# Two transformer-like blocks on one core: gelus in one batch, w8 low parts as differences, three weight pieces prepared at fixed steps

## The chip, the cores and the metric

The kernel runs on one core of a Trainium2 chip (trn2). A core has five engines that run side by side, each with its own queue of instructions: TensorE (PE: matmuls, with PEld for the loads of its weights), VectorE (DVE), ScalarE (ACT), GpSimd (POOL) and SyncE (SP, which here only issues transfers). Data lies in HBM, in SBUF (128 partitions) and in PSUM, where matmuls put their sums in eight banks of 128x512 floats. The metric is the device time of one launch in microseconds; lower is better.

## The reference

All arrays are float32, the sequence has 512 tokens and 1024 channels. The first block (hybrid attention and a gated feed-forward layer) is not touched. What matters of the second block:

```python
h = _rms(x, norm1_w) * (1 + sc1) + sh1
u, q, k, v = split(h @ w_in)                  # 512, 512, 128, 128 columns
# _s5: a state-space scan over the tokens, 32 groups of 16 channels
y = C(scan(u)) + d_skip * u
z = gelu(y)
y_ssm = z * sigmoid(z @ w_glu + b_glu)
# _swa_sink: attention in a window of 128 tokens, 8 q heads, 2 kv heads
y_attn = softmax_with_sink(rms(q) @ rms(k).T + bias) @ v
x = x + g1 * (concat(_rms(y_ssm), _rms(y_attn)) @ w_out)
h2 = _rms(x, norm2_w) * (1 + sc2) + sh2
up = causal_conv3(h2 @ w_up) + conv_b         # 2 x 2816 columns
val, gate = split(up)
x = x + g2 * ((silu(gate) * val) @ w_down)
```

## The kernel before, in words

Activations lie with channels on the partitions and the 512 tokens along them. A product in float32 is made of three matmuls in a faster format (`fp32r`): each operand is split into a high part (`hi`, the rounded value) and a low part (`lo`, the rest), and `mm3` adds hi·hi, hi·lo and lo·hi in PSUM. So each weight has to be split before its use. The weights come in pieces of 128x1024 floats (512 KB), in one queue over the whole kernel: w6 is w_glu (2 pieces here called for by steps `g`), w7 is w_out (8 pieces), w8 is w_up (44 pieces) and w9 w_down.

A piece is prepared by `_Lazy.load` (L366). `fetch` has SP issue the transfer from HBM to a `raw` buffer (L356; there are two, `NRAW`). ACT copies `raw` to `whi`, which rounds it (L374). The low part comes in one of two ways. For weights named in `DMA_LO` (w6, w7 and w8), ACT writes the negated rounded copy to `wlo` (L377) and POOL issues a transfer that fetches the same weights from HBM a second time and adds them to it (L378). For the others, w9 and those of the first block among them, DVE subtracts `whi` from `raw` (L381). There are five `whi` and five `wlo` buffers (`NHL`). A step that uses a piece (`pieces`, `get`) also has the next one loaded (`AHEAD` is 1). Before the second feed-forward block `hold_after` stops this, and `go_on` lets it run again once the normalised halves `hl` are issued (L1366 on ACT, L1367 on DVE).

The first part of the second block interleaves the state-space layer and the attention. The string `ORDER` names its steps one after another, and PE runs them in that order. `a`, `b`, `c`, `d` are the stages of the scan, one number for each quarter of the channels. Step `d` puts a quarter of y in PSUM; `copy("y2", ...)` moves it to SBUF (`ys`, on ACT or DVE by a letter in the string `EN`), eight transfers write it to DRAM in another layout (`d_z`; five of them queued on ACT, three on SP, by `ZQ`), and a transfer on POOL reads it back as `yt`. Step `e` applies gelu to the quarters and splits them into `zhl` (ACT copy L507, DVE subtraction L508): with `EG` at 0, `e0` does quarters 0 and 1 and `e1` quarters 2 and 3. `kp`, `kt`, `qp`, `qt` project and transpose k and q (with a norm: Ln L512, Exp L513, then DVE L533). `s` makes the scores of one window and their softmax (DVE L1598, ACT Exp L1603 and L1605), `t` transposes the probabilities (PE L1616, then a copy `pt`), `v` multiplies by v, and `g` is the gated product with w6 and a tanh (L1643). `R`, `A` are norms, `p` and what follows are the products with w7.

Gelu, tanh and the Ln/Exp pair need different activation tables of ACT. A change of table is an ACT_TABLE_LOAD row; `tables` (L308 to L311) asks for the Ln/Exp table again.

ORDER binds PE alone. The other engines are ordered by a planner that schedules the same instructions by estimated costs, except within `high_priority` and where `issue_after` ties an instruction behind another. So a change in one step moves rows of ACT, DVE, SP and POOL elsewhere.

After the last w7 products `norm_tail` normalises the residual in two halves of the tokens; its square sums end in `rsq` (L519, L520). `start_ffn2` (L1690) then begins the second feed-forward block with three w8 groups, `first8`, in PSUM banks `acc`; later groups go round `tr`, `sc` and `acc`. `conv_ff` (ACT L1717, DVE L1719) takes each group out of PSUM with the causal convolution, `hidden2` applies silu and the product (L1727). w8 and w9 chunks alternate; `d` in `hd` is the hidden layer.

Of the kernel before, what the change touches and what calls it, by code (L numbers as in the profile page):

```python
# [11 lines left out]
AF = mybir.ActivationFunctionType  # L12
# [27 lines left out]
TAIL = 4  # L40
ZQ = "assssaaa"
HP = ""
EG = 0
EN = "avaaavaaaaaaaaaaaaavvvvvvvavavvaaaavaaaaaaaaaaaavaavvvvavvvvaaaavvvvaavvvaaaaavavaaavaavvavvvvvvvvvvavvaavvvvvavvaaavaaaavaaavvaaaaaaavvvvvvvaaaaaaaaavvvavvaavaaaav"
EN_AT = {'k1': (0, 4), 'v1': (4, 4), 'q1': (8, 12), 'h1': (20, 8), 'w1': (28, 8), 's1': (36, 8), 'o1': (44, 16), 't1': (60, 46), 'u2': (106, 4), 'z2': (110, 4), 'y2': (114, 4), 'k2': (118, 2), 'v2': (120, 2), 'q2': (122, 4), 'h2': (126, 12), 's2': (138, 12), 't2': (150, 14)}
ORDER = "U kp0 kp1 a0 a1 kt0 b0 qp0 c0 a2 b1 qp1 kt1 b2 c1 d0 a3 c2 qt0 qt1 b3 c3 d1 s0 qp2 s1 s2 t0 d2 t1 d3 e0 s3 e1 qt2 t2 s4 qp3 v0 t3 s5 v1 g0 qt3 g1 g2 t4 g3 s6 v2 v3 s7 t5 R p0 p1 v4 p2 t6 v5 p3 p4 v6 t7 p5 v7 p6 p7 A"
NW = 16
NHL = 5
SUM_E = "vector"
DMA_LO = ("w6", "w7", "w8")  # L50
LAG = 4
NRAW = 2
NW2 = 19
# [179 lines left out]
def build(tc, I, out, PV, PVN, CS, CSN, CS1, CSN1):  # L233
    nc = tc.nc
    st = ExitStack()
    act = nc.scalar.activation
# [3 lines left out]
    def by(cat, n):  # L240
        o, w = EN_AT[cat]
        assert n < w
        return EN[o + n]

    def copy(cat, n, dst, src, scale=None):

        if by(cat, n) == "a":
            return act(dst, src, AF.Copy) if scale is None else act(dst, src, AF.Copy, scale=scale)  # L248
        if scale is None:
            return V.tensor_copy(dst, src)  # L250
        return V.tensor_scalar(dst, src, scale, None, op0=ALU.mult)
# [8 lines left out]
    def mm(o, l, r, start, stop, **k):  # L260
        nc.tensor.matmul(o, lhsT=l, rhs=r, start=start, stop=stop, **k)  # L261
# [11 lines left out]
    def acc():  # L273
        return pacc.tile([P, 512], F32, tag="acc", name="acc")
# [20 lines left out]
    def V1(n, k=None):  # L295
        o, w = PV[n]
        return pv[:, o:o + w] if k is None else pv[:, o + k:o + k + 1]
# [7 lines left out]
    def tables(after=None, name="natural_log_exp_and_others"):  # L305

        if after is None:
            nc.scalar.preload_act_table_set(name)  # L308
        else:
            with tc.issue_after(after.ins if hasattr(after, "ins") else after):  # L310
                nc.scalar.preload_act_table_set(name)  # L311
# [27 lines left out]
    class _Lazy:  # L339
# [27 lines left out]
        def load(self):  # L367
# [5 lines left out]
            for a, b in self.halves():  # L373
                act(v(hi)[:, a:b], v(raw)[:, a:b], AF.Copy)  # L374
            if self.name in DMA_LO:
                k0, k1, c0, c1 = self.cut
# [7 lines left out]
    wpieces, queue, limit = {}, [], [1 << 30]  # L384
# [113 lines left out]
    def hl():  # L498
        return hlp.tile([P, 2, S], F32R, tag="hl", name="hl")
# [856 lines left out]
    a1 = cpool.tile([P, 16], F32, name="a1")  # L1356
# [36 lines left out]
    a2 = ExitStack()  # L1393
    bp = a2.enter_context(tc.tile_pool(name="attn2", bufs=1, reuse_waits="tile"))

    def wt(nm):
        return bp.tile([P, S], F32, tag="w", bufs=NW2, name=nm)
# [4 lines left out]
    zT, zhl = [], []  # L1402
    zs, z2s, cs, ss, sps, ets, tts, gts = {}, {}, {}, {}, {}, {}, {}, {}

    def s5_load(qs):
        for q in qs:
            ets[q] = tab("et")
            nc.sync.dma_start(ets[q], d_et[q])
            cs[q], ss[q] = wt("co"), wt("si")
            nc.sync.dma_start(cs[q], d_rot[q][:, 0])  # L1410
            nc.sync.dma_start(ss[q], d_rot[q][:, 1])
# [9 lines left out]
    s5_load2((0, 1))  # L1421
    s5_load((2, 3))

    def u_out(q, ps):
        t = wt("uT").rearrange("p (s c) -> p s c", s=8)
        copy("u2", q, t, ps.rearrange("p (c s) -> p s c", s=8))
        nc.scalar.dma_start(d_u[q // 2][q % 2 * 8:q % 2 * 8 + 8].rearrange("g h s c -> (g h) (s c)"), t.rearrange("p s c -> p (s c)"))
# [3 lines left out]
    v2 = bp.tile([P, NT, 128], F32, name="v2")  # L1431
# [15 lines left out]
    def u_last():  # L1447
        for q in range(3):
            u_out(q, group[q][0])
        u_load(0)  # L1450
        ps = acc()
        proj_f(ps, wu[1], h, 1)
        u_out(3, ps)
        u_load(1)
# [25 lines left out]
    def s5_c(q):  # L1480
        if q == 2:
# [8 lines left out]
        V.tensor_tensor(sp[:, :, 1:65], z.rearrange("p (g c) -> p g c", g=8),  # L1490
                        zc.rearrange("p (g c) -> p g c", g=8), op=ALU.add)

    def s5_d(q):
        ut = wt("ut")
        nc.gpsimd.dma_start(ut, d_u[q // 2][q % 2 * 8:q % 2 * 8 + 8].rearrange("g h s c -> (g h) (s c)"))
        py = acc()
        for g in range(8):
            mm(py[:, g * 64:g * 64 + 64], tts[q][:, g * P:(g + 1) * P], ua[:, q * 8 + g], True, False)
            mm(py[:, g * 64:g * 64 + 64], gts[q][:, g, 16:144], sps[q][:, g, 0:64], False, True)
        ys = wt("ys").rearrange("p (g c) -> p g c", g=8)  # L1500
        copy("y2", q, ys.rearrange("p g c -> p (g c)"), py)
        for t in range(8):
            E = {"g": nc.gpsimd, "a": nc.scalar, "s": nc.sync}[ZQ[t]]
            E.dma_start(d_z[q].rearrange("g h t c -> t h g c")[t], ys[16 * t:16 * t + 16])
        yt = xp.tile([P, S], F32, tag="x", name="yt")
        nc.gpsimd.dma_start(yt, d_z[q].rearrange("g h t c -> (g h) (t c)"))
        V.scalar_tensor_tensor(yt, ut, V1("ssm_d", q), yt, op0=ALU.mult, op1=ALU.add)
        zT.append(yt)

    def s5_e(n):  # L1510
        if EG and n == 0:
            return
        for q in (range(4) if EG else (2 * n, 2 * n + 1)):
            ge = act(zT[q], zT[q], AF.Gelu_apprx_tanh)
            zz = hl()
            split(zz, zT[q])
            zhl.append(zz)
        tables(ge)
# [139 lines left out]
    def ssm_out(k):  # L1658
# [5 lines left out]
        V.scalar_tensor_tensor(t, ps, gm[:, k:k + 1], r_s, op0=ALU.mult, op1=ALU.mult)  # L1664
        G.tensor_tensor(x[k], x[k], t, op=ALU.add)

    steps = dict(U=u_last, a=s5_a, b=s5_b, c=s5_c, d=s5_d, e=s5_e, kp=kv_p, kt=kv_t, qp=q_p, qt=q_t,
                 s=swa_s, t=swa_t, v=swa_v, g=glu, R=norm_s, p=ssm_out, A=norm_a)
    with tc.manual_schedule(engines={mybir.EngineType.PE}):
        for step in ORDER.split():  # L1670
            name = step.rstrip("0123456789")
# [71 lines left out]
def _make(inputs):  # L1743
    import concourse.bacc as _bacc

    arrays = arrays_of(inputs)
    PV, PVN = _offsets(pvec(inputs))
    CS, CSN = _offsets(consts_of(False))
    CS1, CSN1 = _offsets(consts_of(True))
    nc = _bacc.Bacc("TRN2", target_bir_lowering=False, num_devices=1)  # L1750
    ins, feed = {}, {}
    for name, a in arrays.items():
        ins[name] = nc.dram_tensor(f"in_{name}_dram", a.shape, F32, kind="ExternalInput").ap()
        feed[f"in_{name}_dram"] = a
    out = nc.dram_tensor("out_0_dram", (D, S), F32, kind="ExternalOutput").ap()
    with tile.TileContext(nc) as tc:
        build(tc, ins, out, PV, PVN, CS, CSN, CS1, CSN1)
    return nc, feed
# [8 lines left out]
```

## Time and profile before

| | |
|---|---|
| three runs | 1284.62, 1287.53, 1288.72 us (median 1287.53) |
| the profiled execution | 1290.43 us, its span 1288.6 us |
| PE busy | 1230.1 us (95%), 6269 matmuls |
| DVE busy | 836.3 us (65%) |
| ACT busy | 553.8 us (43%) |
| POOL busy | 312.1 us (24%) |
| read from HBM | 178.22 MB |

The span is the time between the first and the last instruction of the profiled execution; 1.8 us of its own time lie around it. The busy shares are means over stages that differ: attention of the first block up to some 300 us, its feed-forward layer up to 680, state space and attention of the second block up to about 880, its feed-forward layer after 900. What a stage loses is read in that stage, from the waits of PE.

### The profile page before, as it was taken

To read this page: it belongs to the slowest core of one execution; us is meant where nothing else is said; L and a number is where in the kernel's file an instruction comes from. 1 tells how busy PE (TensorE), PEld (TensorE's weight loads), DVE (VectorE), ACT (ScalarE), POOL (GpSimd) and SP (SyncE) were. 2 spreads that over 40 slices of the span, in tenths; PEclk is the share of its full clock that TensorE was granted. 3 is DMA by queue.
4 is the path that set the end of the run, shared out by engine and by line. 5 is a ranking of instruction groups with operands and counts; after the bars stand their busy time and mean duration, and the time that the engine had idled before them with its cause. 6 is when DMAs were issued, how large, how long until landed. Compare 5 with 4: busy or idle time off the path is not lost.

```text
span 1288.6 us, 17279 instructions
## 1 busy us (share of the span) xinstructions
PE 1230.1 (95%) x6269; PEld 993.0 (77%) x6269; DVE 836.3 (65%) x1622; ACT 553.8 (43%) x918; POOL 312.1 (24%) x399
## 2 busy tenths in 40 slices
PE   7899999999999999999999978889899999999998
PEld 6788765667887878888889877668777788888886
DVE  7668868677977967676667488756547343434362
ACT  6334465454332323232325235765655544444430
POOL 1000004113409283755201331032121211111200
PEclk9999999999999999999999887989899999999999
DMA  6431111126356665666547865457799989796921
GB/s 223 156 112 49 51 33 50 50 61 191 115 162 202 218 200 181 188 194 198 176 144 248 246 150 129 122 129 129 140 209 194 211 168 161 148 177 141 186 82 66
DMA packets 211156, 192.95 MB, mean 150 GB/s; under 512 B 13056, under 2 KB 173712, under 8 KB 211072
## 3 DMA queue, kind: packets, MB, share of 16 engines
q1 hardware_dynamic: 154528, 146.96, 37.8%
q0 software_dynamic: 51456, 40.61, 19.8%
q10 hardware_dynamic: 5088, 4.29, 1.0%
q8 instruction: 50, 0.82, 0.3%
q14 instruction: 34, 0.28, 0.1%
HBM read 178.22 MB, written 15.43 MB: 150 GB/s over the span
## 4 chain that ended last, share of the span: by engine, by line
PE 76%; DVE 9%; issue 5%; DMA 5%; ACT 4%; POOL 1%; SPq 0%; POOLq 0%; DVEq 0%; ACTq 0%
PE acc L261 51%; PE sc L261 12%; PE tr L261 8%; DMA raw<-in_w_dram 3%; PE po L261 2%; DMA wlo<-in_w_dram 2%; DVE wlo L381 1%; PE tr L886 1%; ACT whi L374 1%; DVE z L1478 1%; DVE z L1467 1%; PE tr L1616 1%; DVE z L1466 1%; POOL keep L929 0%; POOL wlo L378 0%
## 5 line engine op out<-in xcount | busy, mean ns | idle before, releaser
L261 PE MATMUL acc<-hl,whi 128*128 128x512 f32 (+1 forms) x1624 | 483.6, 381 | 10.3 <-ACT whi L374 6.1
L374 ACT ACTIVATE whi<-raw 128x1024 fp32r<-128x1024 f32 (+2 forms) x188 | 194.3, 1035 | 392.7 <-PE acc L261 231.4
L261 PEld LDWEIGHTS acc<-hl,whi 128*128 128x128 f32 x1624 | 295.3, 189 | 77.4 <-issue 9.2
L261 PE MATMUL acc<-hl,wlo 128*128 128x512 f32 (+1 forms) x812 | 308.5, 380 | 0.3 <-DMA wlo<-in_w_dram 0.3
L381 DVE TENSOR_TENSOR wlo<-raw,whi 128x1024 fp32r<-128x1024 f32 (+2 forms) x134 | 174.9, 1307 | 67.7 <-ACT whi L374 64.7
L261 PEld LDWEIGHTS acc<-hl,wlo 128*128 128x128 f32 x812 | 153.1, 189 | 31.6 <-issue 3.1
L378 POOL DMA_DIRECT2D wlo<-in_w_dram x54 | 72.0, 1334 | 326.7 <-ACT wlo L377 225.7
L261 PE MATMUL acc<-hd,whi 128*128 128x512 f32 (+1 forms) x472 | 143.1, 386 | 2.1 <-DVE x L1348 2.1
L261 PE MATMUL acc<-whi,hl 128*128 128x256 f32 (+1 forms) x544 | 110.3, 294 | 3.3 <-ACT whi L374 1.7
L261 PEld LDWEIGHTS acc<-hd,whi 128*128 128x128 f32 x472 | 87.0, 188 | 21.6 <-issue 3.1
L261 PEld LDWEIGHTS acc<-whi,hl 128*128 128x128 f32 x544 | 90.0, 197 | 8.8 <-ACT tok L248 3.0
L261 PE MATMUL acc<-hd,wlo 128*128 128x512 f32 (+1 forms) x236 | 91.0, 386 | 0.0
L1082 DVE CUSTOM_DVE_ANT_0 wm<-wm,cb 128x512 f32<-128x512 f32 x96 | 78.0, 844 | 14.3 <-DMA wm<-in_wmod_dram 14.2
L261 PE MATMUL acc<-wlo,hl 128*128 128x256 f32 (+1 forms) x272 | 79.4, 292 | 0.7 <-DVE wlo L381 0.7
L261 PE MATMUL tr<-hl,whi 128*128 128x512 f32 (+1 forms) x240 | 75.2, 397 | 0.0
L261 PE MATMUL sc<-hl,whi 128*128 128x512 f32 x208 | 65.0, 393 | 0.0
L377 ACT ACTIVATE wlo<-raw 128x1024 fp32r<-128x1024 f32 x54 | 56.5, 1045 | 4.8 <-DMA raw<-in_w_dram 2.8
L261 PE MATMUL tr<-hl,wlo 128*128 128x512 f32 (+1 forms) x120 | 48.1, 400 | 8.9 <-DMA wlo<-in_w_dram 8.9
L261 PEld LDWEIGHTS acc<-wlo,hl 128*128 128x128 f32 x272 | 53.8, 198 | 2.5 <-DVE wlo L381 1.0
L929 POOL TENSOR_SCALAR_AFFINE_SELECT keep<-keep 128x128 f32<-128x128 f32 x16 | 9.3, 594 | 185.8 <-ACT keep L923 185.0
L261 PEld LDWEIGHTS tr<-hl,whi 128*128 128x128 f32 x240 | 46.3, 196 | 10.2
L261 PEld LDWEIGHTS acc<-hd,wlo 128*128 128x128 f32 x236 | 44.4, 188 | 9.4
(427 smaller groups left out, 1945.6 us busy)
## 6 DMA issues: line engine op xcount, KB each, us to landing
raw<-in_w_dram SPq DMA_DIRECT2D x176, 512.0 KB, 4.4
wlo<-in_w_dram POOLq DMA_DIRECT2D x54, 512.0 KB, 7.8
wm<-in_wmod_dram SPq DMA_DIRECT2D x96, 256.0 KB, 4.1
xk<-in_xT_dram SPq DMA_DIRECT2D x16, 256.0 KB, 4.6
raw<-in_w_dram SPq DMA_DIRECT2D x10, 256.0 KB, 4.0
d_g<-s5g POOLq DMA_DIRECT2D x4, 576.0 KB, 4.0
gt<-d_g SPq DMA_DIRECT2D x4, 576.0 KB, 6.1
w1c<-in_w1k_dram SPq DMA_DIRECT2D x8, 256.0 KB, 6.1
```

What stands on the lines that cost most here:

```text
L261: nc.tensor.matmul(o, lhsT=l, rhs=r, start=start, stop=stop, **k)
L374: act(v(hi)[:, a:b], v(raw)[:, a:b], AF.Copy)
L377: act(lo[:, :m], raw[:, :m], AF.Copy, scale=-1.0)
L378: nc.gpsimd.dma_start(v(lo), self.src[:, k0:k1, c0:c1], accum_op=ALU.add)
L381: V.tensor_tensor(v(lo)[:, a:b], v(raw)[:, a:b], v(hi.bitcast(F32))[:, a:b], op=ALU.subtract)
L886: nc.tensor.transpose(tp[:, q * P:(q + 1) * P], pr[hh][:, j * P:(j + 1) * P], ident)
L929: G.affine_select(g[:, d], g[:, d], fill=1.0, **past)
L1082: V.tensor_tensor_reduce(wm, wm, cb[:, n * 512:(n + 1) * 512], 1.0, 0.0, ALU.mult, ALU.add, mh[:, n, j:j + 1])
L1466: V.scalar_tensor_tensor(dst[re], src[im], sign, t[im], op0=ALU.mult, op1=ALU.mult)
L1467: V.scalar_tensor_tensor(dst[im], src[re], -sign, t[re], op0=ALU.mult, op1=ALU.mult)
L1478: V.tensor_tensor_scan(z2[:, c], mag8[:, q * 8 + g:q * 8 + g + 1].to_broadcast([P, 64]), z[:, c], 0.0, ALU.mult, ALU.add)
L1616: nc.tensor.transpose(tp[:, m * P:(m + 1) * P], probs[n][:, hh, (j - j0) * P:(j - j0 + 1) * P], ident)
```

## The change

`EG` becomes 1: `e0` returns at once, and `e1` does the four gelus and splits, each gelu tied behind the last copy of a y quarter (`yc[0]`) by `issue_after`. The y copies all go to ACT (the string `EN` had the third on DVE). `w8` leaves `DMA_LO`, so that DVE subtracts for its 44 pieces. Three markers `W` in `ORDER` call `ahead`, which loads the next piece of the queue that is not prepared. Lines after the new functions move by 4 to 7: L1514 is now L1521, L1504 L1510, L1605 L1612, L1643 L1650, L1719 L1726.

```diff
-EG = 0
+EG = 1
-ORDER = "U kp0 kp1 a0 a1 kt0 b0 qp0 c0 a2 b1 qp1 kt1 b2 c1 d0 a3 c2 qt0 qt1 b3 c3 d1 s0 ... p6 p7 A"
+ORDER = "U kp0 kp1 a0 a1 kt0 b0 qp0 c0 a2 b1 qp1 kt1 b2 W c1 d0 a3 W c2 qt0 qt1 b3 W c3 d1 s0 ... p6 p7 A"
-DMA_LO = ("w6", "w7", "w8")
+DMA_LO = ("w6", "w7")
...
+    def ahead():
+
+        next(p_ for p_ in queue if p_.parts is None).load()
+
...
+    yc = [None]
+
     def s5_d(q):
...
-        copy("y2", q, ys.rearrange("p g c -> p (g c)"), py)
+        yc[0] = act(ys.rearrange("p g c -> p (g c)"), py, AF.Copy)
...
         for q in (range(4) if EG else (2 * n, 2 * n + 1)):
-            ge = act(zT[q], zT[q], AF.Gelu_apprx_tanh)
+            with tc.issue_after(yc[0].ins):
+                ge = act(zT[q], zT[q], AF.Gelu_apprx_tanh)
             zz = hl()
...
-    steps = dict(U=u_last, a=s5_a, ...
+    steps = dict(W=ahead, U=u_last, a=s5_a, ...
```

The first place is ACT around the gelus. `yt` is a quarter under gelu, `hl` its high part, `prob` the softmax of a step `s`, `nr` the norm of a tile of q, `d_z` a write of y, `pt` a copy of transposed probabilities. Before:

```order
L512 ACTIVATE nr<-nss,eps 128x8
L1514 ACT_TABLE_LOAD
L1514 ACTIVATE yt<-yt 128x512
L513 ACT_TABLE_LOAD
L513 ACTIVATE nr<-nr 128x8
L1603 ACTIVATE se<-se 128x4
L1605 ACTIVATE prob_7430,sl<-prob_7430,ml 128x256 x4
L507 ACTIVATE hl<-yt 128x512
L1514 ACT_TABLE_LOAD
L1514 ACTIVATE yt<-yt 128x512
```

The same engine after the change, from the last y copy on:

```order
L1507 ACTIVATE ys<-acc 128x512
L1610 ACTIVATE se<-se 128x4
L1612 ACTIVATE prob_7546,sl<-prob_7546,ml 128x256
L1510 DMA d_z_3138<-ys 16x8x64 x4
L1612 ACTIVATE prob_7546,sl<-prob_7546,ml 128x256 x3
L1521 ACT_TABLE_LOAD
L1521 ACTIVATE yt<-yt 128x512 x2
L507 ACTIVATE hl<-yt 128x512 x2
L1521 ACTIVATE yt<-yt 128x512 x2
L507 ACTIVATE hl<-yt 128x512 x2
L311 ACT_TABLE_LOAD
L248 ACTIVATE pt<-tr 128x512
```

The gelus stand together behind the writes of the last y, with one table load ahead and one behind; before they stood in three places with six loads, one pair of them between Ln and Exp of a norm.

The second place is ACT around the first tanh (`sg`), some 20 rows later. `whi` and `wlo` are the split of w7 pieces, `po` and `tot_a` belong to the attention's output. Before:

```order
L1566 ACTIVATE hl<-po,pv 128x256
L377 ACTIVATE wlo<-raw 128x1024
L374 ACTIVATE whi<-raw 128x1024
L255 ACTIVATE sq<-po 128x256
L1643 ACT_TABLE_LOAD
L1643 ACTIVATE sg<-acc,hbg 128x512
L377 ACTIVATE wlo<-raw 128x1024
```

After, from the end of the batch of gelus to the same tanh:

```order
L374 ACTIVATE whi<-raw 128x1024
L512 ACTIVATE nr<-nss,eps 128x8
L377 ACTIVATE wlo<-raw 128x1024
L513 ACTIVATE nr<-nr 128x8
L374 ACTIVATE whi<-raw 128x1024
L377 ACTIVATE wlo<-raw 128x1024
...
L255 ACTIVATE sq<-po 128x256
L1650 ACT_TABLE_LOAD
L1650 ACTIVATE sg<-acc,hbg 128x512
```

Two w7 pieces are split wholly ahead of the tanh; before, the second of them was split around it.

The third place is DVE at the start of the second feed-forward block. `hl` of `hm` are the last normalised halves, `cf` the accumulators taken out of PSUM. Before:

```order
L1367 SCALAR_TENSOR_TENSOR hl<-hm,modT,hl 128x256 x2
L1719 SCALAR_TENSOR_TENSOR cf<-acc,pv,cf 128x511 x2
L1719 SCALAR_TENSOR_TENSOR cf<-acc,pv,cf 128x510 x2
L1719 SCALAR_TENSOR_TENSOR cf<-acc,pv,cf 128x511
L1719 SCALAR_TENSOR_TENSOR cf<-acc,pv,cf 128x510
L1727 TENSOR_TENSOR cf<-cf 128x512
```

After:

```order
L1367 SCALAR_TENSOR_TENSOR hl<-hm,modT,hl 128x256 x2
L381 TENSOR_TENSOR wlo<-raw,whi 128x1024 x2
L1726 SCALAR_TENSOR_TENSOR cf<-acc,pv,cf 128x511 x2
L1726 SCALAR_TENSOR_TENSOR cf<-acc,pv,cf 128x510 x2
L1726 SCALAR_TENSOR_TENSOR cf<-acc,pv,cf 128x511
L381 TENSOR_TENSOR wlo<-raw,whi 128x1024
L1734 TENSOR_TENSOR cf<-cf 128x512
L1726 SCALAR_TENSOR_TENSOR cf<-acc,pv,cf 128x510
```

The subtractions stand in DVE's queue between the instructions that empty PSUM; 44 transfers that added to `wlo` have left the end of POOL's queue.

## Rows read from the trace of the kernel before

**Rows 1.** Windows: start and end, us; busy (count) per engine, PEclk, DMA share, GB/s.

```profile
core 0: us, PE busy (x) PEld busy (x) DVE busy (x) ACT busy (x) POOL busy (x), PEclk, DMA share, GB/s
920.00:1020.00 100.00, 90.07 (x372) 71.68 (x371) 47.08 (x88) 50.07 (x63) 20.43 (x15) 0.95 1.09 206
1020.00:1285.00 265.00, 264.55 (x1144) 214.70 (x1142) 117.38 (x150) 108.31 (x129) 35.93 (x25) 1.00 0.72 144
400.00:640.00 240.00, 239.99 (x1088) 193.97 (x1087) 172.55 (x241) 72.62 (x94) 133.42 (x201) 1.00 0.62 191
794.00:806.00 12.00, 11.08 (x55) 9.46 (x56) 6.42 (x19) 6.54 (x15) 1.07 (x2) 0.53 0.77 180
840.00:844.00 4.00, 2.94 (x9) 2.10 (x10) 4.00 (x17) 3.95 (x11) 0.72 (x1) 0.50 0.46 107
```

**Rows 2.** Waits of PE, 890 to 1288 us: total us, times, longest.

```profile
PE tr L261 <- DMA wlo<-in_w_dram: 8.9, 2, 6.4
...
PE sc L261 <- DMA wlo<-in_w_dram: 0.6, 1, 0.6
```

**Rows 3.** Timeline around the first wait: start, duration; in brackets idle time and its end.

```profile
914.42 0.88 DVE L1367 SCALAR_TENSOR_TENSOR hl<-hm,modT,hl 128x256 fp32r<-128x256 f32 x2 [0.18 <-ACT hl L1366]
...
914.69 1.04 ACT L374 ACTIVATE whi<-raw 128x1024 fp32r<-128x1024 f32 x1
...
916.97 1.44 POOL L378 DMA_DIRECT2D wlo<-in_w_dram  x1 [19.73 <-ACT wlo L377]
...
927.06 0.77 PE L261 MATMUL tr<-hl,wlo 128*128 128x512 f32 x1 [6.43 <-DMA wlo<-in_w_dram]
```

**Rows 4.** Timeline of PE between 785 and 850 us.

```profile
793.04 0.66 PE L1616 MATMUL tr<-cst,prob 128*128 128x128 f32 x4 [1.64 <-DVE pt L250]
...
813.73 1.10 PE L1616 MATMUL tr<-cst,prob 128*128 128x128 f32 x8
...
821.56 0.63 PE L1549 MATMUL tr<-cst,tokn 128*128 128x128 f32 x4 [1.69 <-DVE pt L250]
...
841.06 2.07 PE L261 MATMUL sc<-k2T,q2T 64*128 64x256 f32 x4 [5.04 <-DVE ml L1598]
```

**Rows 5.** Lines, by form, of DVE: 1020 to 1285, then 400 to 680 us.

```profile
L381 DVE TENSOR_TENSOR wlo<-raw,whi 128x1024 fp32r<-128x1024 f32 x20 | 24.3, 1221 | 23.0 <-ACT whi L374 22.7
...
L381 DVE TENSOR_TENSOR wlo<-raw,whi 128x1024 fp32r<-128x1024 f32 x52 | 78.1, 1502 | 10.0 <-ACT whi L374 9.9
```

**Rows 6.** Transfers, 900 to 1012 us: count, KB each, median us to landing.

```profile
raw<-in_w_dram SPq DMA_DIRECT2D x15, 512.0 KB, 8.6
```

**Rows 7.** Timeline in the norm before the second feed-forward block.

```profile
894.47 1.04 ACT L377 ACTIVATE wlo<-raw 128x1024 fp32r<-128x1024 f32 x1
...
897.12 0.42 DVE L520 SCALAR_TENSOR_TENSOR rsq<-sc,rsq 128x256 f32<-128x256 f32 x1 [0.44 <-ACT rsq L519]
```

**Rows 8.** Timeline of ACT around the gelus.

```profile
787.62 1.28 ACT L1514 ACT_TABLE_LOAD   x1
...
789.56 1.28 ACT L513 ACT_TABLE_LOAD   x1
790.85 0.21 ACT L513 ACTIVATE nr<-nr 128x8 f32<-128x8 f32 x1
...
811.34 1.28 ACT L311 ACT_TABLE_LOAD   x1
```

**Rows 9.** Timeline of DVE behind that Exp.

```profile
791.09 0.17 DVE L533 TENSOR_TENSOR nwt<-nr 128x8 f32<-128x8 f32 x1 [0.60 <-ACT nr L513]
...
792.31 0.68 DVE L250 COPY pt<-tr 128x512 f32<-128x512 f32 x1
```

**Rows 10.** Timeline of the fifth w7 piece, ACT and SP.

```profile
826.50 1.05 ACT L377 ACTIVATE wlo<-raw 128x1024 fp32r<-128x1024 f32 x1
...
828.27 0.38 SPq L356 DMA_DIRECT2D raw<-in_w_dram  x1
...
836.36 1.06 ACT L374 ACTIVATE whi<-raw 128x1024 fp32r<-128x1024 f32 x1 [3.57 <-DMA raw<-in_w_dram]
```

**Rows 11.** Waits of PE, 318 to 680 us: total us, times, longest.

```profile
PE acc L261 <- DVE x L1348: 2.1, 2, 1.2
```

More of the change, by code (lines that the diff above doesn't have):

```diff
@@ L42 @@
 HP = ""
-EG = 0
+EG = 1
 EN = "avaaavaaaaaaaaaaaaavvvvvvvavavvaaaavaaaaaaaaaaaavaavvvvavvvvaaaavvvvaavvvaaaaavavaaavaavvavvvvvvvvvvavvaavvvvvavvaaavaaaavaaavvaaaaaaavvvvvvvaaaaaaaaavvvavvaavaaaav"
 EN_AT = {'k1': (0, 4), 'v1': (4, 4), 'q1': (8, 12), 'h1': (20, 8), 'w1': (28, 8), 's1': (36, 8), 'o1': (44, 16), 't1': (60, 46), 'u2': (106, 4), 'z2': (110, 4), 'y2': (114, 4), 'k2': (118, 2), 'v2': (120, 2), 'q2': (122, 4), 'h2': (126, 12), 's2': (138, 12), 't2': (150, 14)}
-ORDER = "U kp0 kp1 a0 a1 kt0 b0 qp0 c0 a2 b1 qp1 kt1 b2 c1 d0 a3 c2 qt0 qt1 b3 c3 d1 s0 qp2 s1 s2 t0 d2 t1 d3 e0 s3 e1 qt2 t2 s4 qp3 v0 t3 s5 v1 g0 qt3 g1 g2 t4 g3 s6 v2 v3 s7 t5 R p0 p1 v4 p2 t6 v5 p3 p4 v6 t7 p5 v7 p6 p7 A"
+ORDER = "U kp0 kp1 a0 a1 kt0 b0 qp0 c0 a2 b1 qp1 kt1 b2 W c1 d0 a3 W c2 qt0 qt1 b3 W c3 d1 s0 qp2 s1 s2 t0 d2 t1 d3 e0 s3 e1 qt2 t2 s4 qp3 v0 t3 s5 v1 g0 qt3 g1 g2 t4 g3 s6 v2 v3 s7 t5 R p0 p1 v4 p2 t6 v5 p3 p4 v6 t7 p5 v7 p6 p7 A"
 NW = 16
@@ L1665, in ssm_out @@
         G.tensor_tensor(x[k], x[k], t, op=ALU.add)
-    steps = dict(U=u_last, a=s5_a, b=s5_b, c=s5_c, d=s5_d, e=s5_e, kp=kv_p, kt=kv_t, qp=q_p, qt=q_t,
+    steps = dict(W=ahead, U=u_last, a=s5_a, b=s5_b, c=s5_c, d=s5_d, e=s5_e, kp=kv_p, kt=kv_t, qp=q_p, qt=q_t,
                  s=swa_s, t=swa_t, v=swa_v, g=glu, R=norm_s, p=ssm_out, A=norm_a)
```

## The prediction

> **What bounds the kernel now.** I read the page's busy shares first, then the windows by stage, then what TensorE (PE) waited for, and last the timelines around each wait. By the page PE is busy for nearly the whole span, so time is to be had only where it stands still or runs at the low level of its clock. Two stretches matter for this change.
>
> The first is the start of the second feed-forward block. From 1020 to 1285 us PE starts 1144 matmuls in 265 us, 0.231 us each, busy for 264.55 of them at a granted clock of 1.00: that stretch is bound by PE itself. From 920 to 1020 us it starts only 372, which at 0.231 us are 85.9 us of work, so 14.1 us are lost there [rows 1]. They are lost twice over: 10 us idle (busy 90.07 of 100), and the rest because part of the matmuls come at the low level of the clock, 1.2 GHz (a granted mean of 0.95 in this stretch) [rows 1]. What PE waited for is one thing: the low parts of w8 pieces that arrive by an adding transfer from HBM, 8.9 us in two waits and 0.6 us in a third [rows 2]. The first wait shows the chain: ScalarE (ACT) has made whi at 915.7 us, writes the negated copy by 916.7, GpSimd (POOL) issues the transfer at 916.97, and the first matmul on wlo starts at 927.06, ten microseconds later [rows 3].
>
> The second stretch is the state-space and attention part, 720 to 850 us, where PE waits for DVE and ACT many times. Three waits touch the change: 1.64 us at 793, 1.69 at 821, and 5.04 at 841 [rows 4]; the transposes of step t3, at 813.73, wait for nothing.
>
> **The w8 low parts.** 44 negating copies leave ACT and 44 adding transfers leave POOL; 44 subtractions come to VectorE (DVE). The trace has that very subtraction, for the w9 pieces of the same block: 1.221 us each [rows 5], so 44 x 1.22 = 53.7 us of DVE. DVE is busy for 117.38 of 265 us in the block from 1020 on [rows 1], 44%, and goes to some 60%.
>
> The Trainium skill, "SBUF — State Buffer", section "SBUF: two separate sides", says that a DVE instruction with two SBUF inputs and a GpSimd instruction that reads SBUF exclude each other for their whole length. The trace agrees in so far as the same subtraction takes 1.502 us in the first block, where POOL computes [rows 5]; by that length the 44 would be 66 us, 65% of DVE, and the sum below would not move.
>
> In place of the ten microseconds from POOL's issue, the low part is then ready one subtraction after whi: the fourth piece has whi at 915.7 and DVE is through with the normalised halves at about 915.3 (0.88 us from 914.42 on) [rows 3], so wlo stands at about 917.0, three microseconds before PE wants it at 920. The fifth piece follows at about 918.4. What is late next is the raw weights: with two raw buffers a piece is loaded when the one before last is split, and PE uses one in 24 x 0.231 = 5.5 us. A raw load of this stage, sharing the transfer engines with the adding ones, needed a median of 8.6 us from its issue [rows 6]; without the adding ones it should need less, and two are under way at a time. So I expect all but half a microsecond of the 14.1 us back: 13.5. Bounds: 6.4 (only the first wait goes, raw is late at the second) and 14.1. Nothing below zero from this part alone, except by the rival on DVE below.
>
> In the norm just before (880 to 905 us) two of the new subtractions fall into a DVE that is almost full: 1.2 us each. The first is absorbed by gaps of DVE there. The second runs beside ACT's square, Ln, Exp and Square, while ACT no longer has the 1.04 us of negation at 894.47 in front of them: rsq, at 897.12 now [rows 7], comes between 0.6 earlier and 1 later. I take 0; bounds -1 and +1.
>
> **The gelus in one batch.** Each change of activation table is a row of 1.28 us on ACT; there are six around the four gelus, first at 787.62, last at 811.34 [rows 8], and in the new order two. That is 4 x 1.28 = 5.1 us of ACT.
>
> The Trainium skill, "ScalarE: Activation LUTs", section "What ACT_TABLE_LOAD costs", puts a switch at 2.66 us, the load and a drain of 1.38. The trace differs: the load at 789.56 lasts 1.28 and the next instruction starts at 790.85 [rows 8], so no drain stands behind it. By the page's figure four switches would be 10.6 us of ACT time; I go by the rows.
>
> What of it lies on the path? At 787.62 load, gelu and load stand between Ln and Exp of the norm of the third q tile [rows 8]; DVE waited for that Exp until 791.09 and with it held the copy of the transposes at 792.31 [rows 9], for which PE waited until 793.04 [rows 4]. In the new order Exp follows Ln at once, about 3.2 us earlier; but DVE has scores and products to do meanwhile, and the copy comes by my count of its queue at about 791.4, 0.9 us earlier.
>
> That gain does not reach far. The last y copy now is in front, and four of the eight writes that carry the fourth quarter to DRAM are queued on ACT behind the softmax of step s3, some 2.5 us later than now. Its gelu, the two copies hl behind it and the load back come first, then the copy pt that step t3 needs: I count 813.8 to 814.4 us for that copy, where PE now passes t3 at 813.73 [rows 4]. So PE waits there some 1.5 us and at qt3 (821) stands where it stands now: 0, bounds -3 and +3.
>
> The larger gain comes from what the new order pulls forward. The splits of the second and third w7 pieces now stand ahead of the tanh instead of around it. In the trace the raw buffer that the fifth w7 piece needs is freed by the negation that ends at 827.5; its load is issued at 828.27, and ACT stands 3.57 us for it at 836.36 [rows 10], with the last two products of the gated step queued behind; DVE and then PE wait for those: the 5.04 us at 841.06 [rows 4]. In the new order that buffer is free at about 820.6 by my count, the load lands before 830, ACT goes on at once, and the last tanh comes about 3.6 us earlier. I take 3.6 us of the 5.04. From 841 to 844 us PE runs at 1.2 GHz, granted 0.50 [rows 1]; if the stall before it shrinks, half of those 3 us comes back too, 1.5. Together 5 us, bounds 0 (the batch is later than I count and uses it up) and 11 (also the low clock from 794 to 806 us goes: 12 us at a granted 0.53 [rows 1] are some 6 us of work at 1.00).
>
> **The three pieces at fixed steps.** Nothing: the rows of ACT at their place are the same in both kernels, and leaving the three markers out of the changed kernel leaves the row order of all five engines as it is. The planner had hoisted these splits already. 0.
>
> **The sum.** -13.5 (w8) + 0 (norm) + 0 (to 821) - 5 (fifth w7 piece) + 0 (pieces) = -18.5 us. The profiled execution took 1290.43 us, span 1288.6 and 1.8 around it, so 1271.9; it lies 2.9 above the median of the runs, 1287.53, so the forecast for a median is 1269.0.
>
> **The rivals.** (a) The attention stage gives nothing: the batch is the new wait, and step t3 and the tanh start as much later as the fifth w7 piece gains. For it: DVE's four splits stand in a row and wait for ACT, with two copies behind them. Against: the splits now behind the tanh cost it 2.1 us less. Time 1287.5 - 13.5 = 1274.
> (b) The clock: shorter waits keep PE at 2.4 GHz from 794 to 806 us, and this stage gives 11: 1287.5 - 13.5 - 11 = 1263. Against: the low level there began after waits of which only one gets shorter.
> (c) The raw loads are late at the second w8 pair, so only 6.4 to 8 us come back in the feed-forward block and little in the attention stage: 1279 to 1281.
> (d) The other side: the subtractions stand in DVE's queue ahead of the evacuations of the accumulators, each waits there for its raw load, and PE runs out of banks. 44 of them cost more than the 18.5 us gained once each holds PE by 0.42 us; at 0.6 us it is +8, 1295.5. For it: a subtraction now stands between two evacuations of the first group. Against, and strongly: the first block does just this, 52 subtractions of 1.5 us from 400 to 680 us with DVE busy for 172.55 of 240 [rows 1, 5], and PE waited for DVE 2.1 us in all from 318 to 680 us [rows 11].
> (e) The change does not do what it says: true of the three pieces, as above, and part of the forecast; for w8 the order shows 44 transfers gone.
>
> **How the numbers follow.** Forecast (1265 to 1273) 42%, (a) 22%, (b) 17%, (c) 10%, no change that a measurement can tell (0.3%, 3.9 us) 4%, slower 5%, of which (d) is nearly all. Faster by over 0.3% is then 91%. The range 1261 to 1278 holds the forecast, (a), most of (b) and a third of (c): 8 in 10.
>
> **What would show it.** Right: from 920 us of now, no PE wait for a transfer wlo, and 0.231 us a matmul from the first 512-column one to the end; two table loads around four gelus; no wait of ACT for raw near the third tanh. Wrong in the first step: PE waits for DVE wlo or for raw in the first 100 us of that block. Wrong in the second: the wait at 841 is still over 3 us, or a new one of over 3 us at the transposes of t3. The forecast is wrong as a whole if PE's matmuls after 1020 us come slower than 0.231 us.

## The result and the profile after

The changed kernel took 1273.72 us (median of 4 runs, 1271.80 to 1277.44) against 1286.22 for the kernel before on the same chip: ratio 0.9882, interval 0.9854 to 0.9909. The ratio, here and below, is an estimate of its own with a 95% interval, and not the quotient of the two medians. The medians lie 12.5 us apart, the interval puts the gain between 12 and 19 us; 1269.0 was forecast. The profiled execution took 1277.44 us, the slowest of its runs and 13.0 less than the one shown of before; its span is 1275.7.

The page of the changed kernel, busy time first and then the two groups of transfers that carry weights in (count, KB, median us to landing):

```profile
PE 1227.8 (96%) x6269; PEld 992.8 (78%) x6269; DVE 890.6 (70%) x1665; ACT 507.7 (40%) x871; POOL 250.4 (20%) x355
HBM read 155.15 MB, written 15.43 MB: 134 GB/s over the span
...
raw<-in_w_dram SPq DMA_DIRECT2D x176, 512.0 KB, 4.3
...
wlo<-in_w_dram POOLq DMA_DIRECT2D x10, 512.0 KB, 7.6
```

DVE has 54.3 us more, ACT 46.1 less, and 23 MB are no longer read twice. The windows of the second feed-forward block, which answer to the first two rows of [rows 1]:

```profile
core 0: us, PE busy (x) PEld busy (x) DVE busy (x) ACT busy (x) POOL busy (x), PEclk, DMA share, GB/s
920.00:1020.00 100.00, 100.00 (x443) 81.66 (x442) 74.24 (x116) 44.12 (x57) 0.00 (x0) 1.00 0.51 145
1020.00:1270.00 250.00, 250.00 (x1082) 203.02 (x1082) 134.48 (x161) 77.16 (x95) 0.00 (x0) 1.00 0.31 91
```

PE is never idle there, at a granted clock of 1.00 throughout: 443 matmuls in the first 100 us instead of 372. The waits of PE from 890 us to the end (total, times, longest) no longer name a transfer, against [rows 2]:

```profile
PE acc L261 <- ACT hl L1366: 2.1, 1, 2.1
PE sc L261 <- DVE sqsum L1342: 0.3, 1, 0.3
```

In the attention stage something else has taken place. PE's waits there, changed kernel, from 785 to 850 us of its timeline (start, duration, in brackets the wait and what ended it), against [rows 4]:

```profile
786.74 1.09 PE L1623 MATMUL tr<-cst,prob 128*128 128x128 f32 x4 [1.26 <-ACT prob L1612]
...
803.96 0.63 PE L1623 MATMUL tr<-cst,prob 128*128 128x128 f32 x4 [1.79 <-DVE q2T L251]
...
817.19 1.97 PE L1623 MATMUL tr<-cst,prob 128*128 128x128 f32 x8 [5.47 <-ACT pt L248]
...
838.04 1.13 PE L261 MATMUL sc<-k2T,q2T 64*128 64x256 f32 x4 [0.87 <-DVE ml L1605]
...
840.90 1.88 PE L261 MATMUL sc<-k2T,q2T 64*128 64x256 f32 x4 [1.73 <-DVE ml L1605]
```

The 5.04 us at 841 have become 0.87 and 1.73, and the waits for pt at 793 and 821 are gone. But step t3, which waited for nothing, now waits 5.47 us. Both places repeat in the other profiles of this study. In the four kernels with the gelus as before, the wait at 841 is 5.04 to 6.76 us and t3 waits for nothing; in the five with the batch in the changed kernel's place, it is 1.73 to 2.36, and t3 waits 2.80 to 5.47 for the copy pt.

Both kernels run 6269 matmuls, in the same order on PE but for a handful around two square sums of the norm. So their starts can be compared number by number, which is finer than windows of equal times. Sorted by start, the time between two of them, in us, is the cost of what lies between. The table has it for every run of the study. Its labels: only_lo and only_g have the w8 part or the gelus of the change alone; first6 and first12 are the kernel before with subtractions for the first six or twelve w8 pieces; the others are the changed kernel with w8 subtracted twice (lo_twice), without the markers (no_w), with the gelus one step later (e_late), with no low part by transfer (no_dma_lo), with both of these, and with later gelus and earlier w7 splits (e_late_early_w7).

```
matmuls              0-700  -4000  -4200  -4300  -4755  -4850  -5120  -6268
before               105.4  670.0   36.1   29.7   72.4   34.5   64.3  265.6
after                107.4  667.6   41.7   25.4   73.6   21.7   62.5  265.6
only_lo              105.0  669.5   36.8   32.0   72.2   21.7   62.5  265.6
only_g               104.6  669.0   39.0   23.6   72.4   34.4   63.9  265.6
first6               106.0  669.2   32.6   30.5   72.2   22.9   67.1  265.6
first12              104.5  666.2   34.6   30.6   72.2   21.7   63.8  265.6
lo_twice             107.3  668.8   39.0   23.4   75.5   22.2   66.2  265.6
no_w                 108.4  668.1   38.7   26.2   72.2   21.7   62.5  265.6
e_late               107.5  669.2   34.0   32.2   72.2   21.7   62.5  265.6
no_dma_lo            106.9  667.5   41.4   26.5   72.2   21.7   62.5  265.6
e_late_no_dma_lo     106.7  666.4   32.9   29.7   72.2   21.7   62.5  265.6
e_late_early_w7      107.5  668.8   34.0   29.2   72.1   21.7   62.5  265.6
```

Matmuls 4000 to 4200 are the gelus and steps t2, t3; 4200 to 4300 the gated products and the wait at 841; 4300 to 4755 the products with w7 and the norm; from 4755 on the second feed-forward block in full width. After against before: +5.6 and -4.3 in the attention stage, which is +1.3; +1.2 around the norm; -12.8 and -1.8 at the start of the feed-forward block; nothing in the last 1148 matmuls. The first two columns hold next to nothing that the change touches, and they differ by up to 4 us from one profile to another. Columns three and four differ by up to 6 between kernels with the same order there (before, first6, first12 and only_lo: 65.8, 63.1, 65.2 and 68.8 together; with the gelus in one batch, only_g, after, no_w and lo_twice: 62.6, 67.1, 64.9 and 62.4). A single profile tells nothing under some 5 us in that stage, so I take the means of each four: column three goes from 35.0 to 39.6 us with the batch, column four from 30.7 to 24.7, +4.6 and -6.0, together -1.5. Part of the spread goes with the clock. From 785 to 850 us the mean granted clock was 0.79 in only_lo, 0.84 in before and 0.89 in first12 and first6, whose gelus stand alike and whose two columns took 68.8, 65.8, 65.2 and 63.1 us. The norm repeats within 1.4 us (after and no_w), the next two columns within 0.1 where all w8 pieces are subtracted once and within 0.4 between before and only_g.

### The profile page after: what moved, and what is told of

Same layout as the page of the kernel before. It is cut to its first block, busy times and chain, and to the rows that moved or that the text cites. A ratio compares the mean times of both kernels' runs of the same rounds, so it can differ in the third digit from the quotient of the medians.

```text
span 1275.7 us, 17117 instructions
## 1 busy us (share of the span) xinstructions
PE 1227.8 (96%) x6269; PEld 992.8 (78%) x6269; DVE 890.6 (70%) x1665; ACT 507.7 (40%) x871; POOL 250.4 (20%) x355
## 4 chain that ended last, share of the span: by engine, by line
PE 80%; DVE 9%; ACT 4%; DMA 3%; issue 3%; POOL 1%; SPq 0%; POOLq 0%; ACTq 0%; DVEq 0%
PE acc L261 52%; PE sc L261 13%; PE tr L261 9%; DMA raw<-in_w_dram 3%; PE po L261 2%; DVE wlo L381 1%; PE tr L886 1%; ACT whi L374 1%; PE tr L1623 1%; DVE z L1482 1%; DVE z L1471 1%; DVE z L1470 1%; POOL keep L929 0%; ACT prob L1612 0%; DVE tokn L540 0%
## 5 line engine op out<-in xcount | busy, mean ns | idle before, releaser
L381 DVE TENSOR_TENSOR wlo<-raw,whi 128x1024 fp32r<-128x1024 f32 (+2 forms) x178 | 231.3, 1301 | 110.1 <-ACT whi L374 105.8
L1082 DVE CUSTOM_DVE_ANT_0 wm<-wm,cb 128x512 f32<-128x512 f32 x96 | 73.8, 801 | 5.9 <-DMA wm<-in_wmod_dram 5.8
L261 PE MATMUL sc<-hl,whi 128*128 128x512 f32 x208 | 64.9, 393 | 0.0
L1348 DVE TENSOR_TENSOR x<-x,acc 128x512 f32<-128x512 f32 (+1 forms) x49 | 31.7, 656 | 22.7 <-PE acc L261 22.7
L261 PEld LDWEIGHTS sc<-hl,whi 128*128 128x128 f32 x208 | 39.1, 188 | 9.0
```

The costliest lines, as they stand in the source:

```text
L381: V.tensor_tensor(v(lo)[:, a:b], v(raw)[:, a:b], v(hi.bitcast(F32))[:, a:b], op=ALU.subtract)
L1082: V.tensor_tensor_reduce(wm, wm, cb[:, n * 512:(n + 1) * 512], 1.0, 0.0, ALU.mult, ALU.add, mh[:, n, j:j + 1])
L1348: done[0] = V.tensor_tensor(x[k][:, cs], x[k][:, cs], ps[:, cs], op=ALU.add)
```

## The experiments

**The w8 low parts alone.** The only edit of the kernel before:

```diff
-DMA_LO = ("w6", "w7", "w8")
+DMA_LO = ("w6", "w7")
```

> The kernel before with one part of the change alone: w8 out of the pieces whose low part comes by an adding transfer; gelus and order as before. Theory: this part is the whole gain, some 14 us at the start of the second feed-forward block, so 1286.2 - 13.5 = about 1272.5, with no PE wait for a transfer wlo behind 900 us. Rival (the parts need each other): under 9 us, above 1277, the rest then belongs to the gelus.

Measured: 1272.21 us against 1287.61, ratio 0.9889 (0.9860 to 0.9919). PE's waits from 880 us on:

```profile
PE acc L261 <- ACT hl L1366: 2.0, 1, 2.0
PE sc L261 <- DVE sqsum L1342: 0.3, 1, 0.3
```

Within the noise this part alone gives what the whole change gives. It does not need the others.

**The gelus alone.** The kernel before with the hunks on EG, `yc` and `issue_after`.

```diff
-EG = 0
+EG = 1
```

> The kernel before with the batch of four gelus alone; w8 as before. Theory: the batch gives back at step t3 what it gains at the fifth w7 piece: 1286 within 2 us, with a PE wait of some 5 us for the ACT copy pt at t3 and no wait of 5 us for DVE ml at 841. Rival (my forecast's step): the fifth w7 piece is a gain of its own, 1281. Second rival: the batch alone is a loss that the w8 part covers in the full change: 1289 or more.

Measured: 1284.87 against 1287.61, ratio 0.9985 (0.9963 to 1.0008): no change that can be told. A gain of up to 4.8 us would fit the interval; the 5 that I had forecast for the fifth w7 piece lie at its edge, just outside. The waits in its trace, 700 us on:

```profile
PE tr L261 <- DMA wlo<-in_w_dram: 8.3, 2, 6.0
...
PE tr L1623 <- ACT pt L248: 4.1, 1, 4.1
...
PE sc L261 <- DVE ml L1605: 2.3, 2, 1.7
```

The wait for pt at t3 has come, the one of 5 us for ml has gone, and w8 waits as before. The first theory holds in its places: the wait at t3 is 4.1 us, and what is left at 841 is 2.3 in two waits (columns three and four: +2.9, -6.1, of which the spread between profiles leaves open how much is real).

**No markers.** The changed kernel with ORDER as before.

```diff
-... b2 W c1 d0 a3 W c2 qt0 qt1 b3 W c3 ...
+... b2 c1 d0 a3 c2 qt0 qt1 b3 c3 ...
```

> The changed kernel without the three markers W. Theory: they do nothing, since the planner prepares these pieces at the same places without them: 1273.7 within 2. Rival: they hold the pieces in place and are part of the gain: 1277 or more.

Measured: 1272.34 against 1287.12, ratio 0.9874 (0.9848 to 0.9900), beside 0.9882 for the changed kernel. The three pieces at fixed steps do nothing that the runs can tell. PE has the changed kernel's order here, and t3 waited 2.80 us in this profile, against 5.47 in the other, so that wait has no fixed size:

```profile
817.05 1.09 PE L1623 MATMUL tr<-cst,prob 128*128 128x128 f32 x8 [2.80 <-ACT pt L248]
```

**Is it latency or load?** Two kernels, with differences for the first six and the first twelve of the 44 pieces, the other parts of the change left out:

```diff
-            if self.name in DMA_LO:
+            if self.name in DMA_LO and not (self.name == "w8" and queue.index(self) < queue.index(wpieces["w8", 0][0]) + 6):
```

> The kernel before, with differences for the first six of the 44 w8 pieces alone; the other 38 keep the adding transfer, the gelus are as before. Theory: the gain lies in the latency of the first pieces, when none is prepared ahead, so six pieces give nearly all of it: 1273 to 1275. Rival: it is the load of 44 extra transfers on the transfer engines, which delays the raw weights through the block: six of 44 give under 4 us, 1282 or more.

> The kernel before, with differences for the first twelve w8 pieces alone, 32 by the adding transfer. Six pieces gave 8.7 us of 15, with the loss back where the seventh piece came by transfer. Theory: the transfer's latency costs only while no pieces are prepared ahead, and after twelve they are: 1272 to 1274, as with all 44. Rival: each change over to the adding transfer costs 3 to 6 us, whenever it comes: 1277 to 1280, as with six.

Measured: 1278.94 against 1287.61, ratio 0.9928 (0.9904 to 0.9952) with six; 1272.49 against 1287.31, ratio 0.9880 (0.9855 to 0.9905) with twelve. With six neither theory held: they give 8.7 us of 15. The timeline of PE in that run shows where the rest is:

```profile
935.27 0.47 PE L261 MATMUL tr<-hl,wlo 128*128 128x512 f32 x1 [0.95 <-DMA wlo<-in_w_dram]
...
947.06 0.47 PE L261 MATMUL acc<-hl,wlo 128*128 128x512 f32 x1 [0.44 <-DMA wlo<-in_w_dram]
...
982.73 0.57 PE L261 MATMUL acc<-hl,wlo 128*128 128x512 f32 x1 [1.96 <-DMA wlo<-in_w_dram]
```

The waits move behind the sixth piece, to pieces that still come by transfer, and with them the stretch from 4850 to 5120 grows to 67.1 us. Twelve pieces get past it: 1.1 us of waiting for wlo in all, and the time of all 44. So the transfers cost at the start, over the first twelve pieces. Behind them 32 transfers of 512 KB cost nothing, and the last 1148 matmuls take 265.6 us with them as without them. I read this as latency that shows as long as PE has caught up with the preparation. The load on the transfer engines fell too: in the changed kernel raw weights land in a median of 4.4 us between 900 and 1012 us, against 8.6 in [rows 6]. Behind the twelfth piece that is no gain of its own; ahead of it latency and load go together, and no run separates them.

**What DVE can carry.** The changed kernel with each w8 subtraction made twice:

```diff
-                for a, b in self.halves():
+                for a, b in self.halves() * (1 + (self.name == "w8")):
```

> The changed kernel with each of the 44 subtractions for w8 made twice, so 54 us more of DVE at 1.22 each, DVE some 70% busy in the second feed-forward block. Theory: they stay beside PE once pieces are prepared ahead; only the two or three pieces at the start, 1.2 us each, can show: 1273.7 plus 0 to 4, at most 1278. Rival (the slower side of my forecast): a subtraction holds the accumulators behind it by 0.4 us or more, then 44 more cost over 17 us: above 1290.

Measured: 1279.93 against 1287.31, ratio 0.9937 (0.9914 to 0.9960), some 6 us more than the changed kernel and 2 more than I allowed. Its windows:

```profile
920.00:1020.00 100.00, 97.05 (x417) 77.36 (x416) 87.75 (x128) 41.90 (x54) 0.00 (x0) 1.00 0.47 139
1020.00:1270.00 250.00, 250.00 (x1082) 203.06 (x1081) 162.19 (x187) 78.82 (x97) 0.00 (x0) 1.00 0.31 92
```

From 1020 us DVE is 65% busy and PE loses nothing. The cost lies at the start, where DVE is 88% busy: 2 to 3 us around the norm, 4 behind it. 44 subtractions cost 6 us, 0.14 each on the mean, and nothing in the last 1148 matmuls; the rival needed 0.4 each.

**Gelus behind the copy that t3 needs.** The changed kernel with the batch one step later:

```diff
-... e0 s3 e1 qt2 t2 s4 ...
+... e0 s3 qt2 t2 e1 s4 ...
...
-            copy("t2", 7 * kv + 2 * i - (i > 0) + j - j0, pt, tp)
+            c_ = copy("t2", 7 * kv + 2 * i - (i > 0) + j - j0, pt, tp)
+            if n == 2 and j == j0:
+                yc[0] = c_
```

> The changed kernel with the batch of gelus one step later: behind step t2, and tied behind ACT's first copy pt of t2 in place of the last y copy, so that this copy no longer stands behind the batch. Theory: the 5.5 us that PE waits for that copy at t3 are a cost of their own; the wait goes and the kernel is 2 to 5 us faster than the changed one, 1269 to 1272 (less than 5.5 where the fifth w7 piece is late again). Rival: what comes later, the gelus' splits and the tanh, sets the end of this stage, and PE only waits elsewhere: 1274 within 1.5.

Measured: 1274.50 against 1287.61, ratio 0.9896 (0.9870 to 0.9922): as the changed kernel, so the rival's time came out. PE's waits from 800 to 850 us:

```profile
PE sc L261 <- DVE ml L1605: 7.1, 2, 5.4
PE tr L1556 <- DVE sl L1613: 2.9, 1, 2.9
PE tr L1623 <- DVE q2T L251: 1.8, 1, 1.8
PE tr L1623 <- DVE prob L1615: 1.4, 1, 1.4
```

The wait of t3 for pt is gone, as meant, and the one at 841 is back with 5.4 us. The planner had moved the w7 splits back around the tanh, and ACT stands for the fifth piece's raw buffer once more:

```profile
837.83 1.06 ACT L374 ACTIVATE whi<-raw 128x1024 fp32r<-128x1024 f32 x1 [3.94 <-DMA raw<-in_w_dram]
```

So the wait at 841 came back together with ACT's wait for the fifth w7 piece, as I had taken it; the edit was not meant to bring it back. The next runs try to remove both.

**Both waits away, by less work on ACT.** The changed kernel with `DMA_LO = ()`, and the same with the later gelus:

> The changed kernel with w6 and w7 made by differences too, so that no low part comes by transfer. 10 negations leave ACT (10 us), 10 subtractions come to DVE, two or three of them in the stage up to 850 us where DVE is at least 70% busy. Theory: ACT's time there is what the fifth w7 piece waits for; raw buffers come free earlier, the batch of gelus is cheaper for what is queued behind it: 1270 to 1272. Rival: in that stage DVE is the tighter engine, the waits of PE for DVE ml grow by 1.2 to 2.5 us: 1275 to 1278.

> The two together: gelus one step later, behind ACT's copy pt of step t2, and w6 and w7 by differences. The run with the later gelus alone took the wait at t3 away and got back a wait of 5.4 us for DVE ml near 841. Theory: that one hangs on the fifth w7 piece's raw buffer, which here comes free without a negation, so both waits go: 1267 to 1270. Rival: it hangs on DVE or on the tanh itself: 1273 to 1276, with the wait at 841 over 3 us.

Measured: 1275.53 against 1287.31, ratio 0.9901 (0.9877 to 0.9925), and 1275.42, ratio 0.9906 (0.9877 to 0.9935). Neither is faster than the changed kernel; each time the rival's time came out. The first did not take the wait at t3 away:

```profile
816.21 1.97 PE L1623 MATMUL tr<-cst,prob 128*128 128x128 f32 x8 [4.82 <-ACT pt L248]
```

In the second both long waits are gone: the longest in the stage is 2.84 us, and the two for ml are 2.40 and 2.35, so its rival had the time right and not the wait of over 3 us. Its profile is the shortest of all (span 1267.8), but it is one of six runs between 1269.55 and 1279.70.

**Both waits away, by order.** The later gelus, three more pieces loaded ahead of step g0, and the tanh tied behind the last negation of them:

```diff
-... t3 s5 v1 g0 qt3 ...
+... t3 s5 v1 W W W g0 qt3 ...
...
-        th_ = act(sg, ps, AF.Tanh, scale=0.5, bias=hbg[:, k:k + 1])
+        with tc.issue_after(neg[0].ins):
+            th_ = act(sg, ps, AF.Tanh, scale=0.5, bias=hbg[:, k:k + 1])
```

> The changed kernel with the gelus behind ACT's copy pt of step t2, as in the run with the later gelus, and with two w7 pieces split wholly ahead of the first tanh (three more pieces loaded ahead of step g0, the tanh tied behind the last negation of them). So both places have the order in which each alone lost nothing. Theory: the batch's cost at t3 (about 5 us) and the fifth w7 piece's wait (about 5 us) are separate, and with both gone the stage from 790 to 850 us is some 5 us shorter than in the changed kernel: 1268 to 1270. Rival: DVE's softmax and splits bound this stage whatever ACT does, the waits turn into waits for DVE: 1272 to 1275.

Measured: 1272.99 against 1287.12, ratio 0.9876 (0.9851 to 0.9901). Both long waits are gone from its trace too; 800 to 850 us:

```profile
PE sc L261 <- DVE ml L1605: 3.6, 2, 2.1
PE tr L1556 <- DVE sl L1613: 2.8, 1, 2.8
PE tr L1623 <- DVE q2T L251: 1.8, 1, 1.8
PE tr L1623 <- DVE prob L1615: 1.4, 1, 1.4
PE acc L261 <- ACT sg L1653: 0.2, 1, 0.2
```

and of its windows the one with the gated products:

```profile
820.00:845.00 25.00, 20.07 (x91) 14.19 (x92) 20.93 (x50) 23.25 (x47) 3.50 (x4) 0.86 0.79 210
```

The rival's time came out: what PE waits for is now mostly DVE, which is 84% busy here, ACT 93%. Matmuls 4000 to 4300 take 63.2 us, within what kernels of either order took (62.4 to 68.8). Taking single waits away from this stage did not shorten it beyond what these runs resolve. I read that as a stage that both engines fill; no run took work from DVE and ACT together, so it is not shown.

No version of these beats the changed kernel by a margin that the runs tell: only_lo, first12, no_w and e_late_early_w7 all lie between 1272.2 and 1273.0.

## Why the prediction was right, and where it was not

**The w8 low parts: right in mechanism and nearly in size.** 13.5 us were forecast, with 14.1 as the upper bound. Matmuls 4755 to 5120 took 98.8 us before and 84.2 after, 14.6 less; at 0.231 us each these 365 matmuls are 84.3, so nothing of the loss is left. The bound was 0.5 short because two of the 372 matmuls counted in its window had begun ahead of 920 us; 370 start in it. DVE's price was as forecast: 54.3 us more in all. Its busy share from 1020 us on is 54% and not some 60, since 23 of the 44 subtractions come before that. The row of after, 1020 to 1272 us, beside the first of [rows 5]:

```profile
L381 DVE TENSOR_TENSOR wlo<-raw,whi 128x1024 fp32r<-128x1024 f32 x41 | 50.2, 1223 | 52.6 <-ACT whi L374 51.0
```

One subtraction took 1.223 us with POOL idle in that stretch, against 1.502 in the first block of the kernel before, where POOL computes [rows 5]. The Trainium skill, "SBUF — State Buffer", section "SBUF: two separate sides", says that a DVE instruction with two SBUF inputs and a GpSimd instruction that reads SBUF exclude each other. Both numbers fit that, though no run here varied POOL's work alone. The fourth and fifth pieces' subtractions came at 917.49, for 2.36 us together, in an execution whose block begins 2.0 us later; PE took up the first of them at 922.45, over three microseconds after it was done, as counted:

```profile
917.49 2.36 DVE L381 TENSOR_TENSOR wlo<-raw,whi 128x1024 fp32r<-128x1024 f32 x2 [0.47 <-ACT whi L374]
```

**The norm: 0 forecast, ±1.** The column from 4300 to 4755 shows +1.2 in the changed kernel, but 72.2 against 72.4 of before in no_w, which has its order, and in only_lo. So it is 0 to about 1; the 1.2 goes with the clock, whose mean from 900 to 910 us was 0.83 in the changed kernel's profile and 1.00 in that of no_w.

**The three pieces: 0, right** (no_w).

**The gelus: the failed step.** I put 0 on the stage up to 821 us and -5 on the fifth w7 piece, and added them up as if the two places did not touch each other. The second place did get shorter: column four went down by 4.3 us in the changed kernel and by 6.0 on the mean of four profiles. The buffer of the fifth w7 piece came free at 822.84 us, 2.2 later than counted, its raw load was issued at 822.86 instead of 828.27, and ACT no longer waited for it. The first term, "PE waits there some 1.5 us and at qt3 (821) stands where it stands now: 0", failed: the wait at t3 was 5.47 us, and matmuls 4000 to 4200 took 5.6 us longer, 4.6 on the mean. That is outside the bounds of 3, and it is the sign that I had named for a wrong second step. I had counted 813.8 to 814.4 us for the copy that t3 needs. It came at 816.54. ACT and SP in the changed kernel:

```profile
800.17 0.60 ACT L1507 ACTIVATE ys<-acc 128x512 f32<-128x512 f32 x1 [2.94 <-PE acc L261]
803.06 0.20 ACT L1610 ACTIVATE se<-se 128x4 f32<-128x4 f32 x1 [2.29 <-DVE se L1609]
803.13 0.31 ACTq L1510 DMA_DIRECT2D d_z<-ys  x1
...
806.61 1.28 ACT L1521 ACT_TABLE_LOAD   x1
807.90 1.15 ACT L1521 ACTIVATE yt<-yt 128x512 f32<-128x512 f32 x2
...
813.55 0.63 ACT L1521 ACTIVATE yt<-yt 128x512 f32<-128x512 f32 x1 [2.94 <-DVE yt L1513]
814.09 1.13 ACT L507 ACTIVATE hl<-yt 128x512 fp32r<-128x512 f32 x2
815.24 1.28 ACT L311 ACT_TABLE_LOAD   x1
816.54 0.60 ACT L248 ACTIVATE pt<-tr 128x512 f32<-128x512 f32 x1
...
822.86 0.33 SPq L356 DMA_DIRECT2D raw<-in_w_dram  x1
...
829.06 0.69 ACT L1650 ACTIVATE sg<-acc,hbg 128x512 f32<-128x512 f32 x1
...
837.92 0.68 ACT L1650 ACTIVATE sg<-acc,hbg 128x512 f32<-128x512 f32 x1
```

The same places before:

```profile
800.20 1.82 ACTq L1504 DMA_DIRECT2D d_z<-ys  x4
...
808.75 0.58 ACT L248 ACTIVATE pt<-tr 128x512 f32<-128x512 f32 x1
...
810.69 0.63 ACT L1514 ACTIVATE yt<-yt 128x512 f32<-128x512 f32 x1 [0.84 <-DVE yt L1507]
...
825.92 0.69 ACT L1643 ACTIVATE sg<-acc,hbg 128x512 f32<-128x512 f32 x1
...
838.41 0.68 ACT L1643 ACTIVATE sg<-acc,hbg 128x512 f32<-128x512 f32 x1
```

Before, the copy pt stood between the third and the fourth gelu; now it stands behind the whole batch. How late the batch comes depends on its last input. Of the eight writes of a y quarter four, and not five, are queued on ACT; `ZQ` has four letters a and four s.

The last y copy ends at 800.77, but its writes on ACT stand behind se, which waits 2.29 us for DVE, and the first goes out at 803.13 instead of 800.20. POOL's read of that quarter is issued at 808.95 instead of 804.24:

```profile
808.95 0.55 POOL L1512 DMA_DIRECT2D yt<-d_z  x1 [8.74 <-DMA x<-d_x]
```

The writes explain 2.9 us of those 4.7; the profile names a load of x, which this read does not use, as the end of its wait, and the rest stays open. The last gelu waits 2.94 us for DVE's step on what was read and starts 2.9 us later than before, with the copies, the load back and pt queued behind. I had named the delay (2.5 us, measured 2.9) and then left it out of the count for pt: the last gelu stood at 810.69 before, so with 2.9 us of delay and 3.0 us of gelu, copies and load behind it pt comes at 816.6, where the trace has it. The delay is not the whole cause. In only_g and lo_twice the last gelu starts 29.2 us after matmul 4000, as before, and t3 still waits 4.1 and 4.0 us: PE gets there earlier, and pt stands behind the batch.

The change was forecast at -18.5 us, and the medians lie 12.5 apart; of the 6 between the two, this step makes 6.3 by the profiles of before and after (+1.3 in place of -5) and 3.5 by the means of four (-1.5). The measured time is the one of rival (a), "the batch is the new wait, and step t3 and the tanh start as much later as the fifth w7 piece gains": it gave 1274, and 1273.72 was measured. Its mechanism is in the rows above: the first tanh comes at 829.06 instead of 825.92, 3.1 us later, and the last at 837.92 instead of 838.41, where I had counted 3.6 earlier. That the forecast still came within 5 us of the median is owed to the w8 term, which is most of the sum.

What bounds the stage stays open. With the wait at t3 taken away as well, the 5 us did not appear (e_late_no_dma_lo, e_late_early_w7): a wait at 841 is not time that comes back when it goes. The forecast had read both numbers of this step, the 0 and the -5, from single waits.

**Other rivals.** (b) The low clock between 794 and 806 us did not go, it came earlier: granted 0.53 from 786 to 796 in the changed kernel. A second low stretch came with the wait at t3 (0.50 from 814 to 820, where it was 1.00 before), and the one behind 841 stayed (0.51 from 841 to 848), so the 1.5 us of clock that I had counted there did not come back. (c) Raw was not late at the second pair of w8 pieces. (d) DVE's queue costs at the start only, and at twice the load. **The tables:** the loads went from six to two, each 1.28 us with the next instruction right behind (806.61, 807.90). The Trainium skill, "ScalarE: Activation LUTs", section "What ACT_TABLE_LOAD costs", gives 2.66 us for a switch, with a drain of 1.38. No such drain stands at these two loads either. The time freed on ACT bought nothing that the runs can tell (only_g). I put that down to the order on ACT, in which a copy that PE needs stands behind the batch; as the later orders bought nothing either, it is not shown.

## What to carry to other kernels

A preparation step that is long in latency cost only where its consumer had caught up with it, at the start of a stage: give the short path to the first pieces and read the gain from the waits there, not from the work saved over the stage. Batching to save table loads puts the whole batch behind its last input; work out when that input comes, with what its own transfers queue behind, and what is queued behind the batch. In a stage where two engines are nearly full, a wait taken away came back as another, so count the stage from one matmul number to another in several runs before believing a gain read from one wait.

## What the runs showed of the hardware

The last 1148 matmuls of the program took 265.6 us in all twelve profiles, with DVE from some 44 to 65% busy, with the extra transfers and without. Against that, the first 700 matmuls, in which nothing differs between the kernels, took from 104.5 to 108.4 us, and the attention stage varied by 5 to 6 us with the same order. Profiles of single executions repeat to a tenth of a microsecond where PE is the bound, and to several microseconds elsewhere. The granted clock goes with these differences: its mean from 95 to 115 us was 1.00 in before, 0.91 in after and 0.83 in no_w, and the first 700 matmuls took 105.4, 107.4 and 108.4 us.
